# A gated-recurrence and gMLP block on one core: TensorE's order bound over four banks, and the gate's transposes written later

## The chip, the cores and the metric

The kernel runs on one core of a Trainium2 chip. The metric is the device time of one execution in microseconds (us). Before the change three runs took 2402.03, 2402.31 and 2403.97 us, a median of 2402.31 us.

## The reference, cut to what matters

One layer over 2048 latent tokens of width 1024 and 256 context tokens. The lines below are those whose products are computed around the change; the second part of the layer (a gated MLP with a 3x3 convolution, width 2816) follows and isn't touched.

```python
h = modulate(rmsnorm(x, norm_mix), sh1, sc1)
p = h @ w_in                      # 3584 columns: forget gates f and b, v, q, output gate, u, v2
q = silu(p_q) * 128 ** -0.5       # 4 heads of 128
o_f, h_f = chunk_gla(q, k_f, v, logf_f, h0_f)        # S_t = diag(f_t) S_(t-1) + k_t v_t^T, o_t = S_t^T q_t
o_b, h_b = chunk_gla(flip(q), flip(k_b), flip(v), flip(logf_b), h0_b)
o = rmsnorm(o_f + flip(o_b), hg_norm)                # per head
o_hg = merge_heads(o) * silu(p_gate)
o_mlp = gelu(u) * (w_spatial @ layernorm(gelu(v2)) + b_spatial)
x = x + g1 * (concat(o_hg, o_mlp) @ w_out)
```

## The kernel before

The sequence is worked in two halves of 1024 tokens. The normalised input of a half is kept on chip, transposed, as a rounded part `xh` and a rest `xl` (8 blocks of 128 channels by 1024 tokens each). For the second half both were stored in DRAM earlier and are loaded over the first half's while its last banks run: sixteen loads of 512 KB from lines 1144 and 1145, the ones for tokens 0 to 511 first.

The projection `h @ w_in` goes by *banks*: 128 output columns by 512 tokens, one PSUM bank of the tag `pj` (three buffers). A bank is 24 matmuls: for each of 8 blocks k the three products `xh*whi`, `xl*whi`, `xh*wlo` (`mm3`; `whi` and `wlo` are the weights' rounded part and rest). The weights of a bank come as one 512 KB load into `raw` (line 211, one buffer at this point), a cast to `whi` on ScalarE (line 222) and a subtraction to `wlo` on VectorE (line 225). The order of the banks is a written list; the second half's begins with `b0`: forward gate and backward gate of head 0, tokens 0 to 511, then both for tokens 512 to 1023. So banks 0 and 2 share one set of weights and banks 1 and 3 the other. Bank 4 is the first of `q0`.

The recurrence of the head before (`hg`) runs between the banks' matmuls, in pieces. After each block k, `slot()` looks whether a piece is due: `later(fn, wait)` notes `T.t + wait`, where `T.t` is a running sum of the time that the written matmuls should take. The pieces that matter here are, in this order: the scores of the level with blocks of 64 (`sc<-Q,K`, 32 matmuls), the transposes of the keys (`mi<-ident,K`, 16), the chunk states (`mi<-vt,kt`, 16), and later the outputs (`mi<-vt,sc` and `mi<-fs,Q`).

What is written is not yet what an engine runs. A scheduler takes the written program and sets each engine's order by its own estimate of when operands are ready; an engine then runs its list strictly in that order. Instructions given to `pin` (`tc.keep_in_program_order`) keep their written order among each other. Before the change TensorE's matmuls of the banks are not pinned.

The output of a head goes through `o_out`: squares on ScalarE, `rstd` on GpSimd, `scaled` (a VectorE multiply to `on`, line 744), and behind it `gated` (four transposes of `on` on TensorE, a VectorE multiply with the gate, line 752, and a store). `scaled` is due 3.2 after the squares, `gated` 2.6 after `scaled`.

Of the kernel before, what the change touches and what calls it, by code (L numbers as in the profile page):

```python
# [50 lines left out]
def view(t, off, dims):  # L51

    return bass.AP(t.tensor, t.offset + off, [list(t.ap[0])] + [list(d) for d in dims])


class Tensor:


    def __init__(self, engine):
        self.engine, self.t = engine, 0.0  # L60

    def matmul(self, out, lhsT, rhs, **kw):
        n = 1
        for _, count in rhs.ap[1:]:
            n *= count
        if lhsT.ap[1][1] < P and out.ap[0][1] == lhsT.ap[1][1]:
            self.t += 2 * (n / 1200 + 0.016) / 4
        else:
            self.t += n / 2400 + 0.0135 if rhs.dtype == F32R else 2 * max(0.112, n / 1200 + 0.005)
        return self.engine.matmul(out, lhsT, rhs, **kw)  # L70

    def transpose(self, out, in_, identity):
        self.t += 0.109
        return self.engine.transpose(out, in_, identity)  # L74


@with_exitstack
def tile_trunk(ctx, tc, x, c, cx, c_ctx, w_ada, b_ada, norm_mix, norm_ffn, w_in, hg_norm, sgu_g, sgu_b,
               w_sp, b_sp, w_out, w_up, conv_w, conv_b, w_down, norm_final, masks, out):
    nc = tc.nc  # L80
    V, S, G, T = nc.vector, nc.scalar, nc.gpsimd, Tensor(nc.tensor)
    ld = nc.sync.dma_start
    st = nc.sync.dma_start
    pin = tc.keep_in_program_order
# [30 lines left out]
    def rstd(pool, ss, n, scale, bias=EPS, keep=lambda i: i):  # L115

        r = pool.tile([P, 8], F32, tag="rs", name="rs", bufs=2)
        keep(G.tensor_scalar(out=r[:, :n], in0=ss, scalar1=scale, scalar2=bias, op0=ALU.mult, op1=ALU.add))
        r2 = pool.tile([P, 8], F32, tag="rs2", name="rs2", bufs=4)
        G.tensor_tensor(out=r2[:, :n], in0=r[:, :n], in1=mhalf[:, :n], op=ALU.pow)  # L120
        return r2
# [53 lines left out]
    hg_q, df_q, bg_q = Pump(), Pump(), Pump()  # L175
# [8 lines left out]
    with es1:  # L184
# [13 lines left out]
        def bank(tag):  # L198
            return ps.tile([P, 512], F32, tag=tag, name=tag, bufs={"pj": 3, "sc": 2, "mi": 3}[tag])
# [38 lines left out]
        def put(dst, src, wait=2.5):  # L238
            hg_q.later(lambda: pin(st(dst, src)), wait)
# [370 lines left out]
        def ctx_state(h, F, K, vt):  # L610
            tot = F
            for B in LV:
                level_update(K, CTX, B, tot, True)
                tot = next_tot(tot, CTX, B)
            yield 9.5
            pt = bank("mi")
            for d in range(2):
                for i in range(2):
                    o = (2 * d + i) * P
                    T.transpose(pt[:, o:o + P], K[:, d, i * P:(i + 1) * P], ident)  # L620
            kt = ph.tile([P, 512], F32, tag="on", name="ckt", bufs=2)
            S.copy(kt, pt)
            yield 2.0
            pd = bank("mi")
            for d in range(2):
                for i in range(2):
                    o = (2 * d + i) * P
                    T.matmul(pd[:, o:o + P], kt[:, o:o + P], vt[:, i * P:(i + 1) * P], start=True, stop=True)
            for d, dst in ((0, hf[h]), (1, hb[h])):
                a, b = (0, 1) if d == 0 else (1, 0)  # L630
                t = ph.tile([P, P], F32, tag="cdh", name="cdh", bufs=2)
                S.copy(t, pd[:, (2 * d + a) * P:(2 * d + a + 1) * P])
                V.scalar_tensor_tensor(out=dst, in0=t, scalar=tot[:, 1 - d, b:b + 1],
                                       in1=pd[:, (2 * d + b) * P:(2 * d + b + 1) * P], op0=ALU.mult, op1=ALU.add)
            yield 0.0

        def need(q, what):
            while what not in done:
                if hg_q.soon:
                    hg_q.flush()  # L640
                    continue
                assert q.tasks
                q.step()

        def marked(g, what):
            yield from g
            done.add(what)
# [10 lines left out]
        for h in range(NH):  # L658
            F, K, vt = sets[h % 2]

            def pre(h=h):
                if h >= 2:
                    need(hg_q, ("ctx", h - 2))
                if h:
                    F, K, vt = sets[(h - 1) % 2]
                    hg_q.add(marked(ctx_state(h - 1, F, K, vt), ("ctx", h - 1)))
# [67 lines left out]
        def o_out(hh, h, g0, o, sg, what):  # L734

            ss = ph.tile([P, 4], F32, tag="oss", name="oss", bufs=4)
            for i in range(4):
                jk = ph.tile([P, P], BF16, tag="ojk", name="ojk", bufs=2)
                S.activation(jk, o[:, i * P:(i + 1) * P], AF.Square, accum_out=ss[:, i:i + 1])
            r = rstd(ph, ss, 4, 1.0 / P)  # L740

            def scaled():
                on = ph.tile([P, 512], F32, tag="on", name="on", bufs=2)
                V.tensor_mul(on.rearrange("p (c q) -> p c q", q=P), o.rearrange("p (c q) -> p c q", q=P),
                             view(r, 0, [[1, 4], [0, P]]))

                def gated():
                    pt = bank("mi")
                    for i in range(4):
                        T.transpose(pt[:, i * P:(i + 1) * P], on[:, i * P:(i + 1) * P], ident)  # L750
                    ot = pm.tile([P, 512], F32, tag="ot", name="ot", bufs=2)
                    V.scalar_tensor_tensor(out=ot, in0=pt, scalar=hgn[:, h:h + 1], in1=sg()[:, g0:g0 + 512],
                                           op0=ALU.mult, op1=ALU.mult)
                    put(oT_d[hh][:, h, g0:g0 + 512], ot, 2.0)
                    if g0:
                        done.add(what)
                hg_q.later(gated, 2.6)
            hg_q.later(scaled, 3.2)

        def chain(states, reverse, h0, tot):  # L760
# [360 lines left out]
        def sequence(hh, names, post):  # L1121
            out_ = []
            for name in names.split():
                two = [part(hh, n) for n in name.split("+")]
                out_ += with_post([b_ for pair in zip(*two) for b_ in pair], post)
                last = name == "q0" if name[1] == "0" and hh else name[0] == "b"
                post = posts[hh, int(name[1])] if last else lambda: None
            return out_, post
# [6 lines left out]
        seq = []  # L1135
# [10 lines left out]

        seq, post = sequence(1, "b0 q0 t0 g0 q1 b1 t1 v0 g1 q2 b2 t2 u0 g2 q3 b3 t3 v1 g3 u1 v2 u2 v3 u3", post)
        first_o = []

        def open_wo():  # L1150
            while hg_q.tasks or df_q.tasks:
                hg_q.flush()
                (hg_q if hg_q.tasks else df_q).step()
            hg_q.flush()
            bg_q.drain()
            hg_q.flush()
            esh.close()
            pw = esw.enter_context(tc.tile_pool(name="pw", bufs=1, side="right", reuse_waits="tile"))
            first_o.append(lambda: pw.tile([P, 2, NK, P], F32R, tag="o", name="o", align_bytes=AL))
            early = len(wo)  # L1160

            def load():
                raw = raw_tile().rearrange("p (k c) -> p k c", c=P)
                ld(raw, oT_d[0][:, :, 0:P])
                wo_early("MM")
                for k in range(early + 1, NK):
                    t = pw.tile([P, 1 if k == early + 1 else 2, D], F32R, name=f"wo{k}", align_bytes=AL)
                    wo_load(t[:, 0, :], key_tile("R", dtype=F32R, name="wo") if k == early + 1 else t[:, 1, :])
                yield 17.0
                o = first_o[0]()  # L1170
                split(o[:, 0], o[:, 1], raw, V, pin)
                first_o.append(o)
                yield 0.0
            bg_q.add(load())
        i = len(seq) - 4
# [687 lines left out]
```

## Time and profile before

| | |
|---|---|
| median of three runs | 2402.31 us |
| the profiled execution: its time / its span | 2400.96 / 2399.2 us |
| TensorE (PE) busy | 2348.0 us, 98% of the span |
| VectorE (DVE) / ScalarE (ACT) / GpSimd (POOL) busy | 1701.7 / 977.2 / 798.7 us |
| mean granted TensorE clock | 0.995 |

All times of day below count from the start of the span. A row of the profile that is in order of time gives start, duration, engine, line and instruction, `out<-in` by the program's names, and in brackets how long the engine had stood idle before it and what ended that. PE rows of neighbouring matmuls overlap, because a matmul's duration includes its way through the array; the distance from start to start is what one costs in a stream. A 128x128 or 32-column product of plain f32 is two records in the trace (64 records for 32 score matmuls, 32 for 16 state matmuls). PEclk 1.00 is 2.4 GHz and 0.50 is 1.2 GHz.

### The profile page before, as it was taken

What the parts mean: (1) busy time and instruction counts of PE and PEld (TensorE: products, weight loads), DVE (VectorE), ACT (ScalarE), POOL (GpSimd) and SP (SyncE); (2) the same over time, 40 slices, a digit from 0 to 9 for tenths busy, and PEclk for the clock granted to TensorE, in tenths of its full rate; (3) what the DMA queues carried; (4) which work ended last, traced back from release to release, by engine and by line L of the source; (5) the groups of instructions that cost most, each with busy time, mean ns of one, the idle gap of its engine ahead of it and who ended that gap; (6) DMA issues with size and microseconds to landing.
All of it is one profiled execution on the core that took longest, in us unless ns stands there. A gap on an engine that the chain in (4) does not pass through costs nothing.

```text
span 2399.2 us, 38712 instructions
## 1 busy us (share of the span) xinstructions
PE 2348.0 (98%) x14951; PEld 1934.5 (81%) x14951; DVE 1701.7 (71%) x2331; ACT 977.2 (41%) x1762; POOL 798.7 (33%) x739
## 2 busy tenths in 40 slices
PE   7999999999999999999999999999999999999998
PEld 5887887878887887887788888888788888888887
DVE  4656667556667753666898787689999984776876
ACT  4664443443445442544433333334333333232343
POOL 0020000000211111003787877878788860000011
PEclk9999999999999999999999999999999999999999
DMA  8364433584445536679522222642222259843744
GB/s 304 121 200 157 141 118 125 173 287 145 161 130 180 176 115 219 208 240 297 171 91 86 83 92 94 254 161 88 90 89 86 88 174 343 269 145 135 250 155 167
DMA packets 305428, 396.39 MB, mean 165 GB/s; under 512 B 33609, under 2 KB 216657, under 8 KB 302557
## 3 DMA queue, kind: packets, MB, share of 16 engines
q1 hardware_dynamic: 301956, 393.17, 49.0%
q8 instruction: 118, 1.93, 0.3%
q10 hardware_dynamic: 3289, 0.76, 0.1%
q14 instruction: 65, 0.53, 0.1%
HBM read 284.73 MB, written 109.13 MB: 164 GB/s over the span
## 4 chain that ended last, share of the span: by engine, by line
PE 50%; POOL 1%; DMA 1%; issue 0%; DVE 0%; ACT 0%; POOLq 0%; SPq 0%; ACTq 0%
PE up L70 33%; PE dn L70 17%; POOL Al L126 1%; DMA raw<-in_w_up_dram 0%; POOL cv L1526 0%; DMA m<-cv 0%; POOL raw L1257 0%; POOL fl L1253 0%; DVE fl L1306 0%; DVE cv L1368 0%; ACT Ah L125 0%; ACT cv L1450 0%; ACT fl L1304 0%; DVE fl L126 0%; PE dn L74 0%
## 5 line engine op out<-in xcount | busy, mean ns | idle before, releaser
L1431 DVE SCALAR_TENSOR_TENSOR dn<-gp,taps,dn 128x1024 f32<-128x1024 f32 x352 | 448.4, 1280 | 14.7 <-ACT dn L1428 11.5
L70 PE MATMUL up<-yfar,Ah 128*128 128x512 f32 x1232 | 394.1, 390 | 0.0
L70 PE MATMUL dn<-thl,mhl 128*128 128x512 f32 x1680 | 381.0, 389 | 0.0
L126 POOL TENSOR_TENSOR Al<-raw,Ah 128x512 fp32r<-128x512 f32 x264 | 342.8, 1309 | 82.0 <-ACT Ah L125 79.4
L70 PEld LDWEIGHTS dn<-thl,mhl 128*128 128x128 f32 x1680 | 315.2, 188 | 65.6 <-issue 0.2
L70 PE MATMUL pj<-xh,whi 128*128 128x512 f32 x896 | 366.9, 410 | 0.0
L70 PE MATMUL pj<-xh,wlo 128*128 128x512 f32 x896 | 351.4, 392 | 2.1 <-DVE wlo L225 2.1
L70 PE MATMUL pj<-xl,whi 128*128 128x512 f32 x896 | 350.3, 391 | 0.0
L125 ACT CAST Ah<-raw 128x512 fp32r<-128x512 f32 x264 | 162.2, 619 | 320.3 <-PE up L70 253.5
L70 PE MATMUL up<-xah,Al 128*128 128x512 f32 x704 | 275.9, 392 | 5.4 <-POOL Al L126 5.4
L70 PE MATMUL up<-xah,Ah 128*128 128x512 f32 x704 | 275.7, 392 | 1.2 <-ACT Ah L125 1.2
L70 PEld LDWEIGHTS up<-yfar,Ah 128*128 128x128 f32 x1232 | 231.6, 188 | 48.1
L70 PE MATMUL up<-xal,Ah 128*128 128x512 f32 x528 | 205.9, 390 | 0.0
L70 PE MATMUL up<-yfar,Al 128*128 128x512 f32 x528 | 205.3, 389 | 0.0
L70 PEld LDWEIGHTS pj<-xh,wlo 128*128 128x128 f32 x896 | 168.2, 188 | 40.1 <-DVE wlo L225 3.6
L70 PEld LDWEIGHTS pj<-xh,whi 128*128 128x128 f32 x896 | 168.5, 188 | 35.2 <-issue 3.5
L70 PEld LDWEIGHTS pj<-xl,whi 128*128 128x128 f32 x896 | 168.8, 188 | 29.1
L70 PE MATMUL dn<-wo,o 128*128 128x512 f32 x768 | 182.7, 394 | 0.8 <-DVE nt L724 0.8
L70 PEld LDWEIGHTS dn<-wo,o 128*128 128x128 f32 x768 | 142.0, 188 | 30.1 <-DVE nt L724 1.0
L70 PEld LDWEIGHTS up<-xah,Al 128*128 128x128 f32 x704 | 132.8, 189 | 34.6 <-POOL Al L126 6.9
L70 PEld LDWEIGHTS up<-xah,Ah 128*128 128x128 f32 x704 | 133.0, 189 | 29.3 <-ACT Ah L125 1.8
L222 ACT CAST whi<-raw 128x1024 fp32r<-128x1024 f32 x68 | 71.4, 1050 | 119.3 <-PE pj L70 96.9
(321 smaller groups left out, 3626.3 us busy)
## 6 DMA issues: line engine op xcount, KB each, us to landing
raw<-in_w_up_dram SPq DMA_DIRECT2D x88, 512.0 KB, 3.6
mr<-m SPq DMA_DIRECT2D x85, 512.0 KB, 4.7
raw<-in_w_in_dram SPq DMA_DIRECT2D x68, 512.0 KB, 3.8
sT<-wd SPq DMA_DIRECT2D x88, 256.0 KB, 5.0
raw<-in_w_ada_dram SPq DMA_DIRECT2D x32, 512.0 KB, 3.6
yfar<-yd SPq DMA_DIRECT2D x14, 1024.0 KB, 16.8
m<-cv SPq DMA_DIRECT2D x22, 544.0 KB, 2.8
raw<-in_w_down_dram SPq DMA_DIRECT2D x22, 512.0 KB, 4.3
```

The lines of the kernel that those rows point to most:

```text
L70: return self.engine.matmul(out, lhsT, rhs, **kw)
L125: keep(S.copy(hi, raw))
L126: (eng or G).tensor_sub(lo, raw, hi.bitcast(F32))
L222: S.copy(hi, raw)
L1431: V.scalar_tensor_tensor(out=cr, in0=gt[:, t // 3:t // 3 + RH, t % 3:t % 3 + GW], scalar=taps[:, t * NF + f:t * NF + f + 1], in1=cr, op0=A ...
```

## The change

Every TensorE instruction that the kernel writes passes through the class `Tensor`; it now hands each one to a function `keep`. That function does nothing, except from the start of bank 0 to the start of bank 4 of the second half, where it is `pin`. So in these four banks the matmuls and all pieces written between them keep the written order on TensorE. Besides, `gated` is due 4.0 after `scaled` instead of 2.6, for all sixteen of its calls.

```diff
@@ -57,7 +57,7 @@
 
 
     def __init__(self, engine):
-        self.engine, self.t = engine, 0.0
+        self.engine, self.t, self.keep = engine, 0.0, lambda i: i
 
     def matmul(self, out, lhsT, rhs, **kw):
         n = 1
@@ -67,11 +67,11 @@
             self.t += 2 * (n / 1200 + 0.016) / 4
         else:
             self.t += n / 2400 + 0.0135 if rhs.dtype == F32R else 2 * max(0.112, n / 1200 + 0.005)
-        return self.engine.matmul(out, lhsT, rhs, **kw)
+        return self.keep(self.engine.matmul(out, lhsT, rhs, **kw))
 
     def transpose(self, out, in_, identity):
         self.t += 0.109
-        return self.engine.transpose(out, in_, identity)
+        return self.keep(self.engine.transpose(out, in_, identity))
 
 
 @with_exitstack
@@ -754,7 +754,7 @@
                     put(oT_d[hh][:, h, g0:g0 + 512], ot, 2.0)
                     if g0:
                         done.add(what)
-                hg_q.later(gated, 2.6)
+                hg_q.later(gated, 4.0)
             hg_q.later(scaled, 3.2)
 
         def chain(states, reverse, h0, tot):
@@ -1147,6 +1147,15 @@
         seq, post = sequence(1, "b0 q0 t0 g0 q1 b1 t1 v0 g1 q2 b2 t2 u0 g2 q3 b3 t3 v1 g3 u1 v2 u2 v3 u3", post)
         first_o = []
 
+        def in_order(keep, pre):
+            def f():
+                T.keep = keep
+                if pre is not None:
+                    pre()
+            return f
+        for i, keep in ((0, pin), (4, lambda i: i)):
+            seq[i] = (*seq[i][:4], in_order(keep, seq[i][4]))
+
         def open_wo():
             while hg_q.tasks or df_q.tasks:
                 hg_q.flush()
```

TensorE at the start of the second half. `pj_5231`, `pj_5328`, `pj_5402` and `pj_5461` are banks 0 to 3; `whi_5070` and `whi_5228` are the two sets of weights. Before, from bank 0's last matmul on:

```order
L70 MATMUL pj_5231<-xh_337,wlo_5071 128x512
L70 MATMUL sc_5352<-Q_4718,K_5315 32x64 x32
L74 MATMUL mi_5426<-ident_60,K_5388 128x128 x4
L74 MATMUL mi_5432<-ident_60,K_5388 128x128 x4
...
L70 MATMUL mi_5473<-vt_3849,kt_5425 128x128 x4
L70 MATMUL mi_5479<-vt_3849,kt_5425 128x128 x4
L70 MATMUL mi_5485<-vt_3849,kt_5438 128x128 x4
L70 MATMUL pj_5328<-xh_337,whi_5228 128x512
L70 MATMUL pj_5328<-xl_336,whi_5228 128x512
```

Now, from the same matmul on:

```order
L70 MATMUL pj_5231<-xh_337,wlo_5071 128x512
L70 MATMUL pj_5328<-xh_337,whi_5228 128x512
L70 MATMUL pj_5328<-xl_336,whi_5228 128x512
L70 MATMUL pj_5328<-xh_337,wlo_5229 128x512
...
L70 MATMUL sc_5352<-Q_4718,K_5315 32x64 x32
...
L70 MATMUL pj_5402<-xh_337,whi_5070 128x512
...
L74 MATMUL mi_5426<-ident_60,K_5388 128x128 x4
L74 MATMUL mi_5432<-ident_60,K_5388 128x128 x4
...
L70 MATMUL mi_5473<-vt_3849,kt_5425 128x128 x4
```

The scores, the transposes of the keys and the first twelve state matmuls stood ahead of bank 1. They now stand behind its 21st matmul, behind bank 2's 21st and behind bank 3's 9th, and bank 1 follows bank 0 at once.

ScalarE at the same place, from the end of bank 0's evacuation. `whi_5228` is the cast of bank 1's weights; `sc_5272` collects the scores, `kt` the transposed keys, `fs` the states. Before:

```order
L574 ACTIVATE K_5225<-pj_5231 128x256
L816 COPY sc_5272<-sc_5352 64x8x64 x2
L585 COPY K_5388<-K_4340 128x8x64
L835 COPY kt_5425<-mi_5426 128x512
...
L855 COPY tb0_3_140<-tot_5392 128x8
L849 COPY fs_5471<-mi_5473 128x512
L222 CAST whi_5228<-raw_5226 128x1024
L849 COPY fs_5471<-mi_5479 128x512
```

Now:

```order
L574 ACTIVATE K_5225<-pj_5231 128x256
L585 COPY K_5388<-K_4340 128x8x64
L855 COPY tb0_3_140<-tot_5392 128x8
L222 CAST whi_5228<-raw_5226 128x1024
L816 COPY sc_5272<-sc_5352 64x8x64 x2
L572 ACTIVATE F_5223<-pj_5328 128x512
L574 ACTIVATE K_5225<-pj_5328 128x256
```

The cast stands directly behind the copies that don't hang on TensorE's moved pieces. The list of SyncE is the same here: the load of `raw_5226`, from which that cast reads, stays behind the sixteen loads of `xh` and `xl`.

TensorE later in the second half, the third and fourth call of `gated` of one head (`mi<-ident,on`) and the scores of its next level. Before:

```order
L74 MATMUL mi_7753<-ident_60,on_7735 128x128 x4
L70 MATMUL pj_7722<-xh_337,whi_7484 128x512
L70 MATMUL pj_7722<-xl_336,whi_7484 128x512
L70 MATMUL pj_7722<-xh_337,wlo_7485 128x512
L70 MATMUL sc_7767<-Q_7498,K_7690 32x32 x32
...
L74 MATMUL mi_7814<-ident_60,on_7748 128x128 x4
```

Now:

```order
L70 MATMUL sc_7768<-Q_7505,K_7681 32x32 x32
L70 MATMUL pj_7764<-xh_337,whi_7457 128x512
L70 MATMUL pj_7764<-xl_336,whi_7457 128x512
L70 MATMUL pj_7764<-xh_337,wlo_7458 128x512
L74 MATMUL mi_7814<-ident_60,on_7745 128x128 x4
...
L74 MATMUL mi_7831<-ident_60,on_7762 128x128 x4
```

The transposes moved behind the scores; counted over all banks the third call stands 12 bank matmuls later than before, and the first such call of the head before (at 648 us in the trace) 6 later.

## Rows read from the trace of the kernel before

**Rows 1.** page, part 1: busy time, share of the span, instructions

```profile
PE 2348.0 (98%) x14951; PEld 1934.5 (81%) x14951; DVE 1701.7 (71%) x2331; ACT 977.2 (41%) x1762; POOL 798.7 (33%) x739
```

**Rows 2.** PE in time order: start us, us, instruction, [idle before <-ended by]

```profile
500.12 0.50 PE L70 MATMUL pj<-xh,whi 128*128 128x512 f32 x1
...
500.70 0.40 PE L70 MATMUL pj<-xh,wlo 128*128 128x512 f32 x1
...
503.26 1.10 PE L70 MATMUL sc<-Q,K 128*32 128x64 f32 x64 [2.17 <-DVE Q L517]
...
506.40 3.25 PE L74 MATMUL mi<-ident,K 128*128 128x128 f32 x16 [2.04 <-DVE K L587]
...
529.75 0.39 PE L70 MATMUL pj<-xh,whi 128*128 128x512 f32 x1
```

**Rows 3.** the same view a head later

```profile
678.97 0.39 PE L70 MATMUL pj<-xh,whi 128*128 128x512 f32 x1
...
689.07 1.99 PE L74 MATMUL mi<-ident,K 128*128 128x128 f32 x16
...
701.98 0.39 PE L70 MATMUL pj<-xh,whi 128*128 128x512 f32 x1
```

**Rows 4.** stretches: length, busy us by engine, granted clock (PEclk), DMA

```profile
48.33:51.74 3.41, 2.53 (x8) 1.66 (x9) 3.41 (x6) 0.00 (x0) 0.00 (x0) 0.50 0.02 5
...
51.74:55.15 3.41, 3.41 (x18) 3.41 (x17) 2.49 (x7) 2.72 (x5) 0.00 (x0) 0.50 0.61 165
...
501.00:512.17 11.17, 6.96 (x105) 6.71 (x104) 5.70 (x10) 8.88 (x17) 2.20 (x1) 0.85 0.77 273
...
505.71:509.13 3.42, 2.73 (x13) 2.76 (x14) 1.33 (x3) 1.71 (x3) 0.00 (x0) 0.50 0.85 289
```

**Rows 5.** SyncE in time order: load of the second bank's weights

```profile
497.73 0.76 SPq L211 DMA_DIRECT2D raw<-in_w_in_dram  x1
```

**Rows 6.** DMA packets by size, 497.7 to 504.8 us

```profile
DMA packets 1478, 2.87 MB, mean 404 GB/s; under 512 B 84, under 2 KB 84, under 8 KB 1477
```

**Rows 7.** DMA packets by size, 504.8 to 508.6 us

```profile
DMA packets 1428, 1.27 MB, mean 335 GB/s; under 512 B 46, under 2 KB 1070, under 8 KB 1427
```

**Rows 8.** ACT in order of time

```profile
511.07 1.05 ACT L222 CAST whi<-raw 128x1024 fp32r<-128x1024 f32 x1
```

**Rows 9.** DVE in order of time

```profile
506.88 0.17 DVE L524 TENSOR_TENSOR tot<-tot 128x16 f32<-128x16 f32 x1
...
512.25 1.22 DVE L225 TENSOR_TENSOR wlo<-raw,whi 128x1024 fp32r<-128x1024 f32 x1
```

**Rows 10.** PE in order of time, at the low clock and after it

```profile
1168.59 0.63 PE L70 MATMUL up<-xah,Ah 128*128 128x512 f32 x1
...
1171.15 0.48 PE L70 MATMUL up<-xah,Ah 128*128 128x512 f32 x1
...
1171.70 0.39 PE L70 MATMUL up<-xah,Al 128*128 128x512 f32 x1
...
1174.43 0.39 PE L70 MATMUL up<-xah,Ah 128*128 128x512 f32 x1
```

**Rows 11.** PE in order of time, its waits from 640 to 740 us

```profile
648.25 0.63 PE L74 MATMUL mi<-ident,on 128*128 128x128 f32 x4 [0.84 <-DVE mv L708]
...
662.14 0.75 PE L70 MATMUL sc<-Q,K 128*32 128x32 f32 x64 [0.75 <-DVE K L593]
...
664.14 1.53 PE L70 MATMUL mi<-wsT,nt 128*128 128x128 f32 x8 [0.36 <-ACT nt L716]
...
734.64 0.63 PE L74 MATMUL mi<-ident,on 128*128 128x128 f32 x4 [0.90 <-DVE on L744]
```

**Rows 12.** DVE in order of time, from one nm row to the next

```profile
651.18 0.16 DVE L714 SCALAR_TENSOR_TENSOR nm<-mv,rs 128x4 f32<-128x4 f32 x1 [1.18 <-POOL rs L120]
...
663.45 0.15 DVE L714 SCALAR_TENSOR_TENSOR nm<-mv,rs 128x4 f32<-128x4 f32 x1
```

**Rows 13.** page, part 6: DMA issues, KB each, median us to landing

```profile
raw<-in_w_in_dram SPq DMA_DIRECT2D x68, 512.0 KB, 3.8
```

## The prediction

> **What bounds the kernel now.** I read the page's busy shares first: TensorE works 2348.0 of 2399.2 us [rows 1], so only its roughly 50 us of idle time can be won, and anything that makes it wait is paid in full. Next came TensorE in order of time around the half's start. Bank 0's last three matmuls start at 500.12 to 500.70; at 0.24 from one to the next the bank's last slot ends at 500.94. Then TensorE stands idle for 2.17 us until VectorE's update of Q allows the scores, and for 2.04 us until the keys allow their transposes; bank 4 starts at 529.75 [rows 2]. The reader is to see two separate things here: 4.21 us of idle time, and between and behind the two waits useful work. From 501.00 to 512.17 TensorE was busy for 6.96 us, although no bank matmul ran [rows 4].
>
> The next view is a stretch that holds the same instructions without a wait: a head later three banks, 32 scores of that level, 16 transposes and 16 state products take from 678.97 to 701.98, 23.01 us [rows 3]. At the half's start they took 529.75 - 500.94 = 28.81. The 5.80 between them are the 4.21 of waits, and mostly the lower clock: 0.50 of the full one from 505.71 to 509.13 [rows 4], in which the 16 transposes ran 3.25 us instead of 1.99 [rows 2, 3].
>
> Third, I asked why those pieces stood ahead of bank 1 at all, and looked for its weights. Their load is issued on SyncE at 497.73 [rows 5], the sixteen loads of the new half before it. It consists of 128 x 8 pieces of 512 B. From 497.7 to 504.8 no packet of that size moves (84 under 512 B, 84 under 2 KB) while the engines move 404 GB/s [rows 6]; from 504.8 to 508.6 there are 1070 - 46 = 1024, the whole load [rows 7]. I take 508.9 for the landing, with 0.3 us for the notice, an estimate. The cast ran at 511.07, late only because ScalarE was busy with the moved pieces' results [rows 8].
>
> **The binding.** It adds no instruction and removes none; it takes away what filled the time until the weights are there. After 500.94 TensorE's next instruction is bank 1's first matmul, which needs `whi`; all that could run is queued behind it on the same engine. Step by step:
> - The load lands at 508.9, since nothing on SyncE or before 501 changes. ScalarE is free by then: the total that its small copy needs is written at 506.88 + 0.17 [rows 9]. Cast 1.05 [rows 8]: 508.9 to 509.95. First matmul at 510.1, after 9.2 us of idle time in place of 4.21.
> - The third matmul needs `wlo`: 1.22 on VectorE [rows 9], so about 511.25. In an unbroken stream it stands 500.70 - 500.12 = 0.58 behind the first [rows 2], so the stream behaves as if it had started at 510.67.
> - From there the same work as in rows 3: 510.67 + 23.01 = 533.68 for bank 4, against 529.75: **+3.93 us**.
> - The clock. It fell in before after 4.21 us of idle time with one piece between; with 9.2 us it falls for certain. After work resumed at 506.40 it stayed low for another 2.7 us; in the longest case it stayed low from 48.33 to 55.15, 6.8 us, with TensorE busy for 2.53 of the first 3.41 [rows 4]. Counted from 510.1 that ends between 512.8 and 516.9, 1.55 to 5.65 us after the third matmul. At the low clock six matmuls take 1171.15 - 1168.59 = 2.56, 0.427 each, behind it twelve take 1174.43 - 1171.70 = 2.73, 0.2275 each [rows 10]: 47% of the time is lost. So 0.7 to 2.65; I take the middle, **+1.7**.
>
> What hides the rest: the scores' copies, the states' chain and bank 4's weights have until 533 and more, and each has several us there, so they cost nothing; if the cover failed, the weights of bank 4 would be first, with one cast and one subtraction, 2.3 us. The part is +5.6, from +4.6 to +6.6.
>
> The Trainium skill, "DMA: Bandwidth & Descriptors", section "Queues, rings and completion order", says that each DMA engine takes the descriptors of a ring in their order. By that a load issued behind the sixteen on the same queue cannot pass them. The trace agrees: the 1024 packets come last [rows 6, 7]. Were it otherwise and the load landed as fast as a usual one, the sum would be the first rival's.
>
> **The later transposes.** TensorE waits at two places before the tail that involve a call of `gated`: 0.84 at 648.25 and 0.90 at 734.64 [rows 11]. The second stands 12 bank matmuls later now, 12 x 0.2275 = 2.7 us, and no long wait follows there: **-0.90**. The first stands 6 later (1.4 us), so it goes as well, but VectorE is next. From the row of `nm` at 651.18 to the next at 663.45 it does 12 us of work without a gap worth naming [rows 12], and at the end of that TensorE waits for it, 0.75 for keys and 0.36 for the rows that follow from `nm` [rows 11]. The same VectorE work stands there now in another order. TensorE arrives 0.84 earlier and waits that much longer: I count **0**. The ends are all three waits gone, -1.95, and a VectorE row more (0.75) ahead of `nm` plus fragments among the scores, +1.0. The two waits behind 900 us in the drain don't move.
>
> **The sum.** 3.93 + 1.7 - 0.9 = +4.7 us on the profiled execution: 2400.96 becomes 2405.7. That execution is 1.35 below the median of the runs, so for the median 2402.31 + 4.7 = **2407.0 us**, 0.2% slower. What follows shifts as a whole: its waits are for work that TensorE's own progress releases.
>
> **Rivals.**
> - *The weights are in time (faster).* If the load landed by 498.7, TensorE would not wait: -5.80 for waits and clock, -0.90 for the gate, 2395.6. The point that decides is the landing. With the usual 3.8 us [rows 13] it lands at 501.5, the first matmul runs at 502.7, the third at 503.85, as if started at 503.3; bank 4 at 526.3 is -3.5, with 0.8 for the clock and -0.9 for the gate -3.6: 2398.7. For it speaks that a scheduler's order is only an estimate; against it rows 6 and 7.
> - *The gate gives more.* All waits of rows 11 go, -2.85, and the clock comes back early, +0.7: 3.93 + 0.7 - 2.85 = +1.8, 2404.1. For it: all four are waits for a chain that gets 1.4 us more. Against it: VectorE's full stretch [rows 12].
> - *The long low clock, and VectorE pays back.* 3.93 + 2.65 at the half's start, and +1.0 - 0.9 at the gate: +6.7, 2409.0. For it: after the longest idle time of the recurrence a partly filled first stretch like that at 48.33 [rows 4].
>
> **How the numbers follow.** My forecast gets 0.60, the weights in time 0.07, the gate 0.18, the long low clock 0.15. About 0.2%, 4.8 us, is what can be told from no change. The forecast lies on that bound: I give half of it, 0.30, to each side. Slower 0.30 + 0.15 = 0.45; same 0.30 + 0.18 + 0.02 (the usual landing) = 0.50; faster 0.05. The range reaches to the two rivals on either side, each with 1 us for the spread of the medians: 2403.1 to 2410.0. The first rival is left out of it; the forecast's own range, from +4.6 - 1.95 - 0.9 to +6.6 + 0.1, is 2404.1 to 2409.0.
>
> **What would show it.** In the profile of the changed kernel: one idle stretch of about 9 us on TensorE from 501, ended by ScalarE's `whi`, and one of about 0.7 by VectorE's `wlo`; the 512-byte packets again at 505 to 508.6; a granted clock of 0.50 over the first matmuls behind it; bank 4 at 535; no wait of 0.9 at the transposes near 740. A landing near 502, or an idle stretch under 5 us there, would make the first part wrong; a wait for VectorE that is gone near 668, or has grown beyond 2 us, the second.

## The result, and the profile after

The changed kernel takes 2414.11 us (median of 6 runs, 2408.57 to 2414.70) against 2403.26 for the kernel before (6 runs, 2402.03 to 2405.32): the ratio is 1.0042, with a 95% interval of 1.0032 to 1.0051. It is 0.4% slower, about 10 us; 2407.0 were forecast, and 2410.0 was the upper end of the range. The profiled execution took 2414.70, its span 2412.9, 13.7 more than the span before.

Busy times hardly moved. The row of the page that answers to [rows 1] (busy us, share, instructions):

```profile
PE 2349.9 (97%) x14951; PEld 1935.9 (80%) x14951; DVE 1704.1 (71%) x2331; ACT 977.4 (41%) x1762; POOL 798.2 (33%) x739
```

TensorE's busy time grew by 1.9 us and the span by 13.7, so most of the loss is time in which TensorE waits; what a low clock costs is inside the busy time (below, a bank matmul of 0.80 us instead of 0.40). To see where, I compared the start of the same bank matmul in the two traces. The columns are its start in the trace before, and how far behind it the other trace stands there; growth from one row to the next is what that stretch cost. Up to 500.70 the instructions are the same, so the 2.8 there is spread from run to run.

```
start before   changed  binding  due 4.0   e13: due 4.0,
               kernel   alone    alone     mix later
500.70          +2.8     +1.9     +1.2      +0.4     end of bank 0
529.75          +9.0     +8.5     +3.2      +1.3     bank 4 starts
656.45          +8.8     +8.5     +3.0      +1.1     before the first head's mix
671.89         +11.8     +8.6     +6.9      +1.1     behind it
773.28         +12.5     +8.4     +8.0      -0.1     ahead of the third head
931.24         +14.0     +7.9     +8.2      -0.9     first matmul of w_out
```

**The half's start.** TensorE in order of time, answering to [rows 2] (start us, us, instruction, idle time before and what ended it):

```profile
503.52 0.40 PE L70 MATMUL pj<-xh,wlo 128*128 128x512 f32 x1
...
512.42 0.80 PE L70 MATMUL pj<-xh,whi 128*128 128x512 f32 x1 [8.50 <-ACT whi L222]
...
513.68 0.80 PE L70 MATMUL pj<-xh,wlo 128*128 128x512 f32 x1
...
520.60 1.10 PE L70 MATMUL sc<-Q,K 128*32 128x64 f32 x64
...
527.21 1.99 PE L74 MATMUL mi<-ident,K 128*128 128x128 f32 x16
...
538.78 0.39 PE L70 MATMUL pj<-xh,whi 128*128 128x512 f32 x1
```

The two waits of 4.21 us are now one of 8.50, ended by `whi`; the scores and the transposes stand behind banks without a wait, and the transposes take 1.99 again. Bank 4 starts 35.26 behind bank 0's last matmul, in place of 29.05 before: +6.2, where the forecast had +5.6.

SyncE, ScalarE and VectorE there, in order of time, answering to [rows 5], [rows 8] and [rows 9]:

```profile
500.82 0.69 SPq L211 DMA_DIRECT2D raw<-in_w_in_dram  x1
```

```profile
511.32 1.04 ACT L222 CAST whi<-raw 128x1024 fp32r<-128x1024 f32 x1 [2.68 <-DMA raw<-in_w_in_dram]
```

```profile
512.40 1.23 DVE L225 TENSOR_TENSOR wlo<-raw,whi 128x1024 fp32r<-128x1024 f32 x1 [3.98 <-ACT whi L222]
```

The load is issued 2.70 ahead of bank 0's last matmul (2.97 before) and released the cast at 511.32, for which ScalarE sat idle 2.68. The cast's 1.04 and `wlo`'s 1.23 follow as forecast. Two stretches (length, busy us by engine, granted clock, DMA), the first answering to the low one of [rows 4]:

```profile
508.52:518.76 10.24, 6.30 (x14) 4.57 (x15) 2.45 (x2) 1.17 (x2) 0.00 (x0) 0.50 0.69 223
...
675.78:679.19 3.41, 3.41 (x10) 2.75 (x10) 3.41 (x6) 2.12 (x3) 0.00 (x0) 0.50 0.00 0
```

The clock is 0.50 (1.2 GHz) for 10.24 us, up to 5.1 us behind the third matmul: near the long end of the forecast (5.65). The second stretch, 0.50 for 3.4 us more, has no counterpart in the trace before.

**The heads behind it.** TensorE, answering to the waits of [rows 11]:

```profile
663.27 0.66 PE L74 MATMUL mi<-ident,on 128*128 128x128 f32 x4 [0.77 <-DVE ot L752]
...
671.27 0.60 PE L70 MATMUL sc<-Q,K 128*32 128x32 f32 x46 [0.28 <-DVE K L593]
...
673.67 0.49 PE L70 MATMUL mi<-wsT,nt 128*128 128x128 f32 x2 [1.79 <-ACT nt L716]
...
674.09 0.27 PE L70 MATMUL sc<-Q,K 128*32 128x32 f32 x8
...
675.50 0.58 PE L70 MATMUL pj<-xh,whi 128*128 128x512 f32 x1
...
678.43 0.63 PE L70 MATMUL pj<-xh,whi 128*128 128x512 f32 x1
...
750.44 0.63 PE L74 MATMUL mi<-ident,on 128*128 128x128 f32 x4 [1.37 <-DVE on L744]
```

The wait ahead of `mi<-wsT,nt`, the product that I call the mix, has grown from 0.36 to 1.79. The order is another one, too: the scores are cut at 46 of 64, and the other 18 matmuls lie between those of the mix. In the trace before all 64 scores ran, then three bank matmuls, then the mix. Two rows of these three, not shown before, in the trace of before:

```profile
662.82 0.50 PE L70 MATMUL pj<-xh,whi 128*128 128x512 f32 x1
...
663.39 0.39 PE L70 MATMUL pj<-xh,wlo 128*128 128x512 f32 x1
```

From 663.39 to the mix at 664.14 less 0.36 TensorE worked. In the changed kernel nothing of the kind is left between the scores and the mix; the bank matmuls come from 675.50 on, and at 678.43 they run 0.63 long, at the low clock. And the wait of 0.90 on the second head's transposes did not go: it is 1.37.

VectorE and GpSimd ahead of the mix; the first row answers to the second of [rows 12]:

```profile
672.96 0.16 DVE L714 SCALAR_TENSOR_TENSOR nm<-mv,rs 128x4 f32<-128x4 f32 x1 [0.30 <-POOL rs L120]
```

```profile
669.44 3.48 POOL L120 TENSOR_TENSOR rs<-rs,mhalf 128x4 f32<-128x4 f32 x1
```

`nm` came 3.35 behind the last `mv` row in the trace before and comes 4.06 behind it now, waiting for a GpSimd step on 128x4 values that took 3.48 us (1.33 before; the GpSimd step ahead of it took 1.07 before and 0.19 now).

### The profile page after: what moved, and what is told of

It reads as the page before. It is cut to its first block, busy times and chain, and to the rows that moved or that the text cites. A ratio compares the mean times of both kernels' runs of the same rounds, so it can differ in the third digit from the quotient of the medians.

```text
span 2412.9 us, 38706 instructions
## 1 busy us (share of the span) xinstructions
PE 2349.9 (97%) x14951; PEld 1935.9 (80%) x14951; DVE 1704.1 (71%) x2331; ACT 977.4 (41%) x1762; POOL 798.2 (33%) x739
## 4 chain that ended last, share of the span: by engine, by line
PE 45%; DVE 6%; POOL 1%; issue 1%; DMA 1%; ACT 0%; SPq 0%; POOLq 0%; ACTq 0%
PE up L70 27%; PE dn L70 17%; DVE dn L1440 3%; DVE edges L1445 1%; POOL Al L126 0%; DVE gp L1524 0%; DMA xn<-cv 0%; POOL raw L1266 0%; DMA m<-cv 0%; DVE cv L1532 0%; POOL fl L1262 0%; DVE fl L126 0%; DVE keep L1518 0%; POOL cv L1535 0%; DVE fl L1315 0%
```

## Experiments

Each kernel was timed against the kernel before on the same chip; "us" is the ratio times that kernel's median (2401.5 to 2403.4).

**Which part costs (e1, e2).** The binding alone (the changed lines of `Tensor` and of the sequence, with `gated` at 2.6), and the due alone:

```
-                hg_q.later(gated, 2.6)
+                hg_q.later(gated, 4.0)
```

> The binding alone, gate's transposes due at 2.6 as before. Theory A (the binding costs the wait for bank 1's weights, and the later due of gate's transposes costs the rest by itself): about +6 us against the kernel before (5 to 7.5): TensorE idles 8 to 9.5 us at the half's start until ScalarE has cast the 512-byte columns, the granted clock is low for 10 us after it, and from bank 4 on each bank matmul stands the same distance behind the kernel before, to the end; the waits of 640 to 840 us are those of the kernel before. Theory B (the binding's delay and low clock also upset the stretch after it, the due of 4.0 is worth nothing or the 0.9 us that was forecast): +9 to +12 us, with the growth between 640 and 840 us that the changed kernel shows.

> The due of 4.0 alone, nothing bound at the half's start. Theory A: +3 to +5.5 us against the kernel before; bank 4's first matmul stands where it does in the kernel before, and the distance then grows between 640 and 840 us, with waits of over 1 us on the transposes' copy at the banks where the deferred state products are also written later. Theory B: -1 to +1 us, with no such growth. The forecast on record had -0.9 for this part.

Measured: binding 1.0020 (1.0012 to 1.0029), +4.8 us; due 1.0031 (1.0020 to 1.0042), +7.4. Together 1.0051, against 1.0042 (1.0032 to 1.0051) for the changed kernel: the parts add within the intervals, and theory B falls. Each part lies a little outside the range that theory A gave it (+5 to +7.5 and +3 to +5.5). The binding alone (TensorE in order of time) waits as the changed kernel does, and its waits of 640 to 780, 0.81, 0.75, 0.37 and 0.87, are those of [rows 11]:

```profile
502.62 0.40 PE L70 MATMUL pj<-xh,wlo 128*128 128x512 f32 x1
...
512.05 0.80 PE L70 MATMUL pj<-xh,whi 128*128 128x512 f32 x1 [9.03 <-ACT whi L222]
...
513.31 0.80 PE L70 MATMUL pj<-xh,wlo 128*128 128x512 f32 x1
```

The due alone shows the cut scores, the wait and the bank matmul at the low clock, and two stretches:

```profile
665.47 0.60 PE L70 MATMUL sc<-Q,K 128*32 128x32 f32 x46 [0.29 <-DVE K L593]
...
667.48 0.53 PE L70 MATMUL mi<-wsT,nt 128*128 128x128 f32 x2 [1.41 <-ACT nt L716]
...
667.94 0.34 PE L70 MATMUL sc<-Q,K 128*32 128x32 f32 x8
...
672.05 0.63 PE L70 MATMUL pj<-xh,whi 128*128 128x512 f32 x1
```

```profile
667.73:674.56 6.83, 6.83 (x35) 5.21 (x35) 4.27 (x7) 3.30 (x7) 0.00 (x0) 0.51 0.22 76
...
504.00:514.24 10.24, 7.75 (x92) 7.54 (x93) 3.00 (x5) 6.02 (x13) 1.53 (x1) 0.50 0.65 233
```

From 656.45 to 671.89 it loses 3.9 us (table). The 6.83 us at 0.51 are 3.2 of that, by the 47% of [rows 10]; the wait, longer by 1.41 - 0.36 where the wait for the scores is shorter by 0.75 - 0.29, makes the rest. The second stretch is a caution: at the half's start, where this kernel's instructions are those of before, the clock was low for 10.24 us and not 3.42. That is the +2.0 of the table's second row, and spread, no effect of the edit. Kernels e6, e7, e8, e13 and e14, all unchanged there, had the low clock for 6.8 us and lose about 1 us to the trace before in that stretch too; against such a start the binding costs some 5, which is what its runs measure.

**Is it the late weights (e3, e4)?** One load is written earlier, behind the first eight of the half's sixteen token loads, alone (e3) and with the binding (e4):

```
+             if q:
+                 load_raw((HW, 512))
              ... the eight loads of token 512 on
```

> The kernel before with one load moved: bank 1's 512-byte columns of the weights are read right behind the first two token loads of the half, ahead of the other eight token loads; nothing is bound. If the late weights are what holds the half's start in either order (theory A), the wait at the half's start goes wholly or mostly: TensorE's first 12 bank matmuls are followed by the next bank in its written place, and the kernel comes out 3 to 7 us under the kernel before. Rival: the eight token loads that now land about 1.3 us later are what the transposes wait for, and the time stays within 1 us of the kernel before.

> The same moved load together with the binding. Theory A: the binding costs only by the weights' lateness, so with the weights early this stands with the kernel that only moves the load, within 1 us of it, and 9 to 13 us under the binding alone. Rival: an order held word for word costs something by itself (a transpose that may not slip in where TensorE waits), and this stays 1 us or more above the kernel that only moves the load.

Measured: 0.9972 (0.9962 to 0.9982), -6.7 us, and 0.9974 (0.9965 to 0.9983), -6.2. TensorE of e3:

```profile
500.63 0.40 PE L70 MATMUL pj<-xh,wlo 128*128 128x512 f32 x1
...
500.86 0.40 PE L70 MATMUL pj<-xh,whi 128*128 128x512 f32 x1
...
505.75 1.10 PE L70 MATMUL sc<-Q,K 128*32 128x64 f32 x64
...
512.36 2.00 PE L74 MATMUL mi<-ident,K 128*128 128x128 f32 x16
...
523.92 0.39 PE L70 MATMUL pj<-xh,whi 128*128 128x512 f32 x1
```

Bank 1 follows bank 0 at the usual 0.23, and the scores and the transposes stand in their written places with nothing bound. The binding costs only by the weights' lateness; with the weights early it costs nothing that these runs tell (0.5 us between the two). Bank 4 starts at 523.92, 5.8 ahead of the trace before: the 5.80 that the prediction read as waits and clock.

**What in the due of 4.0 costs (e5 to e8).** The kernel before has 4.0 for the step of `deferred`, 7.0 for `mix`. e5 changes the first alone, e6 and e7 change one of them besides the due of 4.0, and e8 gives the due of 4.0 to a part of the calls:

```
e5  deferred:  yield 4.0 -> 5.4                    (gated stays 2.6)
e6  deferred:  yield 4.0 -> 2.0                    gated 4.0
e7  hg_q.later(mix, 7.0) -> 7.3                    gated 4.0
e8  hg_q.later(gated, 2.6 if hh else 4.0)
```

> The kernel before, gate's transposes due at 2.6, with one number of deferred changed: the step ahead of its state products waits 5.4 instead of 4.0, so that these products stand where the changed kernel has them (behind bank matmuls 1809, 1815, 2070, 2073, 2337, 2343 instead of 1803, 1806, 2061, 2064, 2331, 2334); the scores' last quads of 666 us stay whole ahead of the mix. Theory A1 (the products come so late that their sums reach VectorE behind the scores' updates, and the copy for the transposes behind POOL's two steps): +3 to +6 us against the kernel before, with the waits on the transposes' copy grown as in the changed kernel. Theory A2 (the scores' last quads that the later due put between the mix's matmuls hold everything up at 670 us, and the clock falls there): 0 to +1.5. Theory A3 (the transposes' own lateness costs, by the banks of PSUM that they hold): -1 to +1.

> The due of 4.0 for gate's transposes, with the step ahead of deferred's products shortened from 4.0 to 2.0, so that the products stand where the kernel before has them or 3 to 6 bank matmuls earlier; the scores' quads stay whole ahead of the mix. Theory A1: -2 to +1 us against the kernel before, 6 us or more under the due of 4.0 alone. Theory A2: the same, -1 to +1.5. Theory A3: +5 to +9, as the due of 4.0 alone.

> The due of 4.0 as in the changed kernel, nothing bound, and the due of the mix 7.3 instead of 7.0: the mix's eight matmuls then stand three bank matmuls later (1872), behind all of the scores' quads, and the products of deferred stay late (1809, 1815; the next head's at 2064, 2067 instead of 2070, 2073). Theory A2: -1 to +2 us against the kernel before, without the wait of over 1 us and the low clock at 665 to 680 us. Theory A1: +3 to +7, nearly all of the due of 4.0 alone. Theory A3: the same as A1.

> The due of 4.0 for deferred's calls alone, 2.6 for the own ones: deferred's first products stand where the kernel before has them (1803, 1806), those of the second head late (2070, 2073), and the scores' quads of 670 us lie between the mix's matmuls. Theory A2: +4 to +9 us against the kernel before, with the low clock at 665 to 680 us. Theory A1: +1 to +4, the growth only from the second head (730 to 860 us) on. Theory A3: about half of the due of 4.0 alone, +3 to +5.

Measured: e5 1.0021 (1.0011 to 1.0031), +5.0; e6 1.0003 (0.9994 to 1.0011), +0.7; e7 0.9986 (0.9977 to 0.9995), -3.4; e8 1.0017 (1.0008 to 1.0027), +4.1. Numbers of bank matmuls in these texts leave out the first 384 of the trace (up to 102.3 us). Theory A3 falls with e7: its transposes stand within 6 bank matmuls of where the changed kernel has them, and it is no slower than before; e6 comes out as A1 and A2 have it. e7's -3.4 is below A2's range too, for a reason that the next group shows. A2 holds in e8, which has the cut scores, a wait of 2.03 ahead of the mix and 3.4 of its loss between 656 and 672:

```profile
666.42 0.49 PE L70 MATMUL mi<-wsT,nt 128*128 128x128 f32 x2 [2.03 <-ACT nt L716]
```

A1 holds in e5 by its time, but not by its place: e5 loses only 0.5 there, and 3.5 between 773 and 931, at the third head. TensorE, GpSimd, VectorE and the stretch:

```profile
828.76 1.09 PE L74 MATMUL mi<-ident,on 128*128 128x128 f32 x4 [3.12 <-DVE on L744]
```

```profile
818.40 0.19 POOL L118 TENSOR_SCALAR rs<-oss 128x4 f32<-128x4 f32 x1 [14.94 <-ACT ojk L739]
...
822.77 4.03 POOL L118 TENSOR_SCALAR rs<-oss 128x4 f32<-128x4 f32 x1 [3.09 <-ACT ojk L739]
```

```profile
821.86 2.21 DVE L517 TENSOR_TENSOR Q<-Q,F 128x1024 f32<-128x1024 f32 x1
...
824.52 1.10 DVE L593 TENSOR_TENSOR K<-K,F 128x512 f32<-128x512 f32 x1
825.54 1.20 DVE L524 TENSOR_TENSOR tot<-F 128x1024 f32<-128x1024 f32 x1
```

```profile
828.16:834.98 6.82, 6.21 (x79) 4.87 (x80) 6.82 (x11) 1.69 (x3) 0.00 (x0) 0.53 0.83 269
```

The GpSimd step between the squares and the copy takes 0.19 us at 818.40 and 4.03 at 822.77, beside VectorE's updates of Q, K and the totals, and ends at 826.80, where the last of them ends at 826.74; the copy comes late, TensorE waits 3.12, and the clock goes to about half. So late products can cost by themselves where, as in e5, the transposes are not moved with them. What they make of the changed kernel's loss is not shown: e7 and e13 have the products of the first and the third head behind the same bank matmuls as the changed kernel, and lose at most 0.4 us there against the trace before (from 656 to 672, and from 773 to the last bank matmul at 929.10).

**Does moving the mix undo it (e9 to e15)?** e7's trace gains 2.1 us between 57 and 188 us, in the first half, where `gated` is not called. So the mix was moved alone, and by halves:

```
e9   changed kernel,  mix 7.3      e13  gated 4.0, mix 7.3 if hh else 7.0
e10  before,          mix 6.8      e14  before,    mix 7.0 if hh else 7.3
e12  before,          mix 7.3      e15  before,    mix 6.8 if hh else 7.0
```

> The changed kernel whole, with the mix due at 7.3 instead of 7.0, so that its matmuls stand behind all of the scores' quads. Theory A2 (the gate part costs because the scores' last quads fall between the mix's matmuls): what the binding alone costs less what the due of 4.0 with the later mix gives, 5.5 - 3.4 = +2 us against the kernel before (0 to +4), and 8 to 11 under the changed kernel. Rival (the two parts do not add: the binding's delay sets the stretch after it): within 3 us of the changed kernel, +8 to +12.

> The kernel before, gate's transposes due at 2.6, and the mix due at 6.8 instead of 7.0: the first head's transposes and state products stay where they are (1776 to 1830; 1803, 1806), but the scores' last quads now fall between the mix's matmuls (1866), and the second head's products stand 6 bank matmuls later. Theory A2: +3 to +6 us against the kernel before, with a wait of over 1 us ahead of the mix and a low clock behind it at 662 to 675 us. Theory A1 (only late products cost): 0 to +4, with the growth behind 730 us.

> The kernel before with the mix due at 7.3 alone, gate's transposes at 2.6. It splits the -3.4 of the due of 4.0 with the later mix: if the later transposes are worth something by themselves, this stands within 1 us of the kernel before; if the later mix gives it all, at -2.5 to -4.5.

> The due of 4.0 with the mix at 7.3 in the second half alone; the first half, where gate has no transposes, keeps 7.0. The profiles of the two runs with the mix at 7.3 throughout stand 2.1 us ahead already at 188 us, in the first half, so that their times do not tell what the later mix undoes of the due of 4.0. Theory A2 (the later due of the transposes costs by where the mix of 666 us then stands): -1 to +2.5 us against the kernel before, 5 to 8 under the due of 4.0 alone, with no low clock at 665 to 680 us. Rival B2 (the first half gave it all): +4 to +7.

> The kernel before with the mix at 7.3 in the first half alone, all of the second half as before. A2: -1.5 to -4 us, all of what the later mix gives by itself: the wait of 2.4 us on xk's transposes at 186 us goes. B2: the same. If it is under 1 us, the gain of the later mix alone came from the second half.

> The kernel before with the mix at 6.8 in the second half alone: the scores' quads of 666 us between the mix's matmuls, and the second head's state products 6 bank matmuls later, with the first half as before. If those quads between the mix's matmuls are what costs, +3 to +5 with a low clock at 660 to 675 us; if only the wait ahead of the mix counts, which in the earlier mix throughout was 1.23 us where the kernel before has 0.75 and 0.36 in two pieces, +0 to +1 there, and what else comes stands at 737 to 750 us behind the late products, +3: together +3 to +5 too, told apart by the stretch.

Measured: e9 1.0005 (0.9996 to 1.0014), +1.2; e10 1.0034 (1.0022 to 1.0046), +8.2; e12 0.9984 (0.9975 to 0.9993), -3.8; e13 0.9994 (0.9985 to 1.0002), -1.4; e14 0.9994 (0.9985 to 1.0003), -1.4; e15 1.0022 (1.0013 to 1.0031), +5.3. In e9 the parts add, as its theory has it. e12 gives all of e7's -3.4 without the later transposes, so these add nothing that the two runs tell.

e13 against e2 is the test that settles most: the same due of 4.0, the first half untouched, and the 7.4 us are gone. TensorE of e13, two stretches, and the GpSimd step:

```profile
663.57 0.75 PE L70 MATMUL sc<-Q,K 128*32 128x32 f32 x64 [0.29 <-DVE K L593]
...
664.25 0.50 PE L70 MATMUL pj<-xh,whi 128*128 128x512 f32 x1
...
664.82 0.40 PE L70 MATMUL pj<-xh,wlo 128*128 128x512 f32 x1
...
665.97 1.54 PE L70 MATMUL mi<-wsT,nt 128*128 128x128 f32 x8 [0.75 <-ACT nt L716]
...
736.59 0.60 PE L74 MATMUL mi<-ident,on 128*128 128x128 f32 x4
...
826.60 0.63 PE L74 MATMUL mi<-ident,on 128*128 128x128 f32 x4 [1.89 <-DVE on L744]
```

```profile
664.00:670.83 6.83, 6.08 (x62) 4.79 (x52) 6.52 (x13) 3.97 (x8) 1.23 (x1) 1.00 0.29 98
...
826.00:832.80 6.80, 6.20 (x90) 5.20 (x91) 6.80 (x11) 2.88 (x5) 0.00 (x0) 1.00 0.89 273
```

```profile
661.75 3.48 POOL L120 TENSOR_TENSOR rs<-rs,mhalf 128x4 f32<-128x4 f32 x1
```

All 64 scores run, three bank matmuls follow, and the mix waits 0.75, although the GpSimd step is as slow here (3.48) as in the changed kernel. The clock stays at 1.00. The transposes at 736.59 find their copy ready: the 0.90 of [rows 11] goes, as the prediction had it, and from 716 to 773 e13 gains 1.2. Not all of the difference to e2 is the mix itself. At 656 to 672 it is 3.9 of the 7 or so that the two traces part from bank 4 on; the rest lies in the second and third heads, where the mix's new place also brings the second head's state products forward by 6 bank matmuls, so there the two causes are not separated.

e15 does the reverse: transposes and products of the first head as before, the mix earlier.

```profile
667.03 0.49 PE L70 MATMUL mi<-wsT,nt 128*128 128x128 f32 x2 [1.91 <-ACT nt L716]
...
741.32 1.09 PE L74 MATMUL mi<-ident,on 128*128 128x128 f32 x4 [2.28 <-DVE on L744]
```

```profile
667.03:673.86 6.83, 6.83 (x45) 5.62 (x46) 5.53 (x9) 3.56 (x7) 0.00 (x0) 1.00 0.06 22
740.94:744.35 3.41, 3.03 (x66) 2.49 (x67) 2.23 (x3) 1.47 (x3) 2.54 (x3) 0.50 0.69 216
```

The wait ahead of the mix is 1.91, and from 656 to 672 it loses 1.1; the clock did not fall there. The cut scores thus cost about 1 us by the wait, and the 3 or 4 of e2 and e8 only with the fallen clock; why the clock fell there and not here stays open. Its larger loss comes at 741, behind products 6 bank matmuls late, with the clock at 0.50 for 3.41 us.

e14 has the first half's share: the wait of 2.38 on `xk`'s transposes (before, first row) is 0.19 (e14, second):

```profile
186.28 0.30 PE L74 MATMUL mi<-ident,xk 128*128 128x128 f32 x1 [2.38 <-DVE xk L253]
```

```profile
185.90 0.30 PE L74 MATMUL mi<-ident,xk 128*128 128x128 f32 x1 [0.19 <-DVE xk L253]
```

Its trace gains 2.1 us between 57 and 188 us, but its time is not told from the kernel before. e10's time is above every expectation; in its trace 4.2 of it stand ahead of 500.70 already, and the growth behind is as in e15 (+4.6 from 529.75 to 931.24, and +5.1 there).

**Two candidates (e11, e16).** Both have the load of e3:

```
e11  gated 4.0, mix 7.3        e16  gated 2.6, mix 7.0 if hh else 7.3
```

> Candidate that may beat both kernels: nothing bound, bank 1's 512-byte weight columns read ahead of the half's other token loads, gate's transposes due at 4.0, the mix at 7.3. If the gains add: -6.8 (the load) - 3.4 (due and mix) = -10 us against the kernel before (-8 to -12). If they do not: -6 to -7, as the load alone.

> Candidate: the 512-byte weight columns read early and the mix at 7.3 in the first half alone, gate's transposes at 2.6 and the second half's written order untouched. If the two gains add: -6.8 - 3 = -10 us against the kernel before (-8 to -12). If the later transposes are worth something once the mix stands later, this stays 1 to 3 us above the candidate that has the due of 4.0 too.

Measured: e11 2389.99 us, 0.9945 (0.9932 to 0.9957), -13.2; e16 2394.57, 0.9961 (0.9947 to 0.9974), -9.4. Both are faster than both kernels; for e11 the two gains added would make -10.1, and its interval reaches from -16.3 to -10.3; each of the two gains is itself known to some 2 us only. Whether the due of 4.0 is worth something once the mix is out of its way stays open: e13 says nothing measurable, and the intervals of e11 and e16 overlap.

## Why the prediction was wrong, point by point

- *What bounds the kernel, and the late weights:* right. One idle stretch of 8.50 us ended by `whi`, the clock at 0.50 behind it, bank 4 at +6.2 by profile (4.6 to 6.6 forecast; some 5 against a start with the usual low stretch), +4.8 us by the runs of the binding alone. The third matmul stands 10.16 behind bank 0's last, where 511.25 - 500.70 = 10.55 was the forecast. Of that forecast the 0.3 us for the notice of the landing is a term that no row shows by itself; the landing released the cast 7.80 behind bank 0's last matmul, where 8.2 was the forecast.
- *The first call of `gated`, "I count 0":* this is the step that failed. With the second call it put the whole part at -0.9, and the due alone measured +7.4. It let only the transposes move and weighed VectorE's work in another order. The written order is made by due times that count TensorE's own written time, so later transposes also shift what is due behind them: the scores' step came three bank matmuls later while the mix stayed, and both fell into one slot. The prediction saw "fragments among the scores" and gave them at most +1.0; they cost +3.0 in the changed kernel (the waits grew by 1.0 together, and 3.41 us at half the clock make 1.6 by the 47% of [rows 10]) and +3.9 alone, because TensorE's cover between the scores and the mix went and the clock fell. e13 shows that with the cover back the loss is gone.
- *The second call, "-0.90":* failed as well. The products from which the copy is made moved too, here by 9 bank matmuls where the transposes moved by 12, and the wait became 1.37; from 672 to 773 the changed kernel loses 0.7 in place of a gain. "No long wait follows there" was read from where the transposes now stand, not from where their input comes from. In e13, with the products 6 bank matmuls earlier than in the changed kernel, the 0.90 does go.
- *What follows shifts as a whole:* wrong by another +1.5 at the third head (773 to 931), where the forecast had no change. The changed kernel has waits of 1.00, 1.08 and 0.29 there (before 0.29, 0.66 and 0.58), 0.8 more. e5 shows that late products can cost there, but e13, with products as late, loses only 0.3 up to the last bank matmul, so the cause of the +1.5 stays open.
- *The rivals:* none had a loss of this size on the gate's side; the worst had +1.0.

The slow GpSimd step bears on both places, the mix and the late copies. GPSIMD Engine Reference of the Trainium skill, section "Key points", says that GpSimd shares its SBUF interfaces with VectorE and contends with VectorE instructions that have two inputs in SBUF. The rows agree (0.19 us, and 4.03 beside such updates, in e5), but no run took VectorE's work away to show it.

## What to carry to other kernels

Where the order is written by due times, a step that is moved moves its neighbours: compare the whole order, each waiting instruction with what stands ahead of it and where its input is made, before a wait is booked as won. A product that waits for another engine's chain needs other TensorE work ahead of it, and on an idle stretch of 1.4 us among short instructions the clock can cost more than the wait. And where work was pulled forward because a load is late, move the load; binding the order only makes the lateness visible.

## What the runs showed that was not expected

- The clock fell to 0.51 behind a wait of 1.41 us ahead of the mix (e2, 667.73 to 674.56), and stayed at 1.00 behind a wait of 1.91 in e15 at 667 and one of 1.89 in e13 at 826.60.
- For the same instructions at the half's start the low stretch was 3.42 us in one execution and 10.24 in another, 2 us of time between them.
- One GpSimd instruction on 128x4 values took 0.19 to 4.03 us, another 1.01 to 3.48.
